# The token scales move into a filler tile, and the attention's operand comes first in its pool

## The chip, the cores and the metric

The kernel runs on one core of a Trainium2 chip. The metric is the time of one execution on the device, in microseconds (us). The time before is the median of three runs.

## The reference

A small decoder trunk on 256 tokens of width 2048, all in float32, with two layers and one shared key and value side:

```
h = x
h = h + chunked_gmlp(rmsnorm(h), w_in, w_s, w_out)        # layer 0: 2048 -> 4096, gelu, mix in chunks of 128 tokens, 2048 -> 2048
h = h + conv_ffn(rmsnorm(h), w_up, conv, w_down)          # 2048 -> 11264, causal conv of width 3, silu(gate) * value, 5632 -> 2048
k, v, c = fox_shared_kv(h, w_kvf)                         # 2048 -> 4112: keys, values, cumulative forget gates
h = h + forgetting_attention(rmsnorm(h), w_qg, w_out)     # layer 1: q and gate 2048 -> 4096, 16 heads of 128, 2048 -> 2048
h = h + conv_ffn(rmsnorm(h), w_up, conv, w_down)
out = rmsnorm(h)
```

## The kernel before

Every weight matrix is read once from HBM, in chunks of 128 x 1024 float32 (tile raw). A product keeps float32 accuracy by splitting both sides into a rounded part and a remainder in the format fp32r: ScalarE (ACT) rounds a chunk into whi, VectorE (DVE) writes the remainder into wlo, and an activation tile holds both parts side by side, 2 x 256 values for each of its 128-row slices. Three products are summed in PSUM: rounded by rounded, rounded by remainder, remainder by rounded. Class Stream runs the chunks in one written order: a chunk is loaded six ahead and split three ahead of its matmuls, and the steps of other work (generators) are advanced between chunks. So the order of instructions on every engine is fixed by the code.

There are two forms of matmul blocks, and they differ in what streams through the TensorE array and what is held in it as weights:

- feat_block (the gMLP's u and output a_out, the FFN's up, the gate b_g and the attention's output b_out): whi or wlo is held, 128 x 128 at a time, and the activation tile streams, 256 columns at a time. The tile is X1 for most, mlp_X2 for a_out, att_X2 for b_out.
- tok_blocks, short_block, with_forget and seven_block (a_in_v, b_q, the key, value and forget projections kvf, the FFN's down): the activation tile is held and whi or wlo streams, mostly 256 columns at a time. The tile is X1 for a_in_v and b_q, att_X2 for kvf, ffn_H for down.

All these matmuls go through the helper mm (line 227). A few after each call of between() are 512 columns wide.

Tiles get their place in a partition's memory from pools, stacked in the order in which each pool is opened and each tile first asked for, in steps of 32 bytes: first const (col, spare, X1, acc, rB, scales, ident, ones), then wpool (4 whi, 4 wlo, 4 raw, of 4352, 4352 and 4096 bytes), then small (place, which nothing uses, ones_r, sq and small things), then one phase pool at a time: mlp, ffn0, att, ffn1. In wpool a block form begins its data at FEAT_AT = 0 or TOK_AT = 32 elements, 0 or 128 bytes into whi and wlo.

The token scales (rcol, two columns of scales) are made by token_sums; token_rows turns them with a DVE transpose (128 x 32) and sends them through DRAM to rB, which has them along the row. In the last down block of layer 0, fourth is the first to ask for a tile of the att pool: it uses the front of att_v as scratch.

Start addresses in the built program before, bytes in each partition:

```
X1 7520   whi 43008, 47360, 51712, 56064   wlo 60416, 64768, 69120, 73472   raw 77824, ...
mlp_X2 99392   ffn0_H, ffn1_H 99392   att_v 99392   att_turned 115776, 117824   att_gain 119872   att_X2 119904
mlp_wr 164992   mlp_vr 169088   parts_qk 217056 and 219104
```

Of the kernel before, what the change touches and what calls it, by code (L numbers as in the profile page):

```python
# [10 lines left out]
F32 = mybir.dt.float32  # L11
# [6 lines left out]
P = 128  # L18
# [170 lines left out]
def build(ctx, tc, d, out):  # L189
    nc = tc.nc  # L190
    ctx.enter_context(tc.manual_schedule())
    const = ctx.enter_context(tc.tile_pool(name="const", bufs=1))
    wpool = ctx.enter_context(tc.tile_pool(name="wpool", bufs=AHEAD + 1))
    small = ctx.enter_context(tc.tile_pool(name="small", bufs=1))
# [8 lines left out]
    X1 = const.tile([P, KD, 2 * T], F32R, name="X1")  # L203
    acc = const.tile([P, T], F32, name="acc")
    rB = const.tile([P, T], F32, name="rB")
    scales = const.tile([P, 32], F32, name="scales")
    rcol = scales[:, :2]
    ident = const.tile([P, P], F32, name="ident")
    ones = const.tile([P, 2], F32, name="ones")

    small.tile([P, 144], F32, name="place")
    ones_r = small.tile([P, 2], F32R, name="ones_r")
    s = Stream(nc, wpool)
    ph = Phase(tc)
# [140 lines left out]
    def token_rows(key):  # L355

        way = dram.tile([1, T], F32, name=f"way_r{key}")
        turned = small.tile([P, 32], F32, name="turned_r", tag="turned_r")
        nc.vector.transpose(turned, scales)
        yield  # L360
        for g in range(4):
            nc.gpsimd.dma_start(way.rearrange("o (t g i) -> (o t) g i", t=2, g=4)[:, g, :],
                                turned[32 * g:32 * g + 2, :])
        yield
        yield
        nc.gpsimd.dma_start(rB, way[:1, :].to_broadcast([P, T]))

    def token_scale():
        yield
        token_sums()  # L370
        yield
        yield from token_rows("b")
# [274 lines left out]
    def sums_apart(blk):  # L647


        box = {}  # L650

        def sums(m):
            box["m"] = m
            if blk == 3:
                yield from residual_prepared()
                return
            Y = ph.temp("apart", [P, 4, T], bufs=1)
            nc.scalar.activation(Y[:, 1, :], m[:, 0, :T], AF.Copy)
            yield
            nc.vector.tensor_tensor(Y[:, 0, :], Y[:, 1, :], m[:, 0, T:], op=OP.add)  # L660
            nc.vector.tensor_tensor(Y[:, 3, :], Y[:, 0, :], m[:, 1, T:], op=OP.subtract)
            yield
            nc.vector.tensor_tensor(Y[:, 0::2, :], m[:, 1:, :T].to_broadcast([P, 2, T]), Y[:, 0::3, :], op=OP.subtract)
            box["Y"] = Y

        def fourth(ps):
            m, Y = box["m"], att("v")[:, 0, :CHUNK].rearrange("p (a b) -> p a b", a=4)
            nc.scalar.activation(Y[:, 1, :], m[:, 0, :T], AF.Copy)
            yield
            nc.vector.tensor_tensor(Y[:, 0, :], Y[:, 1, :], m[:, 0, T:], op=OP.add)  # L670
            nc.vector.tensor_tensor(Y[:, 3, :], Y[:, 0, :], m[:, 1, T:], op=OP.subtract)
            nc.vector.tensor_tensor(Y[:, 0::2, :], m[:, 1:, :T].to_broadcast([P, 2, T]), Y[:, 0::3, :], op=OP.subtract)
            Z = [Y[:, 2 * tb:2 * tb + 2, :].rearrange("p a b -> p (a b)") for tb in range(2)]
            for tb in range(2):
                nc.vector.tensor_tensor(Z[tb], Z[tb], ps(tb, 0, 512), op=OP.add)
            for tb in range(2):
                yield
                turned = blocks_turned(Z[tb].rearrange("p (h x) -> p h x", h=4))
                yield
                s.start(rows_added(blk, tb, rows_out(f"d{blk}{tb}", turned), Z[tb]))  # L680

        def done(ps):
            if blk == 3:
                yield from fourth(ps)
                return
            while "Y" not in box:
                yield
            for tb in range(2):
                z = box["Y"][:, 2 * tb:2 * tb + 2, :].rearrange("p a b -> p (a b)")
                nc.vector.tensor_tensor(z, z, ps(tb, 0, 512), op=OP.add)  # L690
                yield
                turned = blocks_turned(z.rearrange("p (h x) -> p h x", h=4))
                yield
                s.start(rows_added(blk, tb, rows_out(f"d{blk}{tb}", turned), z))
                yield

        return done, sums

    def rows_added(blk, tb, way, place):
        out_for, in_for = (2, 4) if blk == 3 else (3, 5)  # L700
        for _ in range(out_for):
            yield
        rows = place.rearrange("p (r x) -> p r x", r=4)
        rows_in(rows, way)
        for _ in range(in_for):
            yield
        hh = h[:, 4 * blk:4 * blk + 4, tb * P:(tb + 1) * P].rearrange("p h (r j) -> p r h j", r=4)
        nc.vector.tensor_tensor(hh, hh, rows.rearrange("p r (h j) -> p r h j", h=4), op=OP.add)
        state["added"] += 1

    def residual_prepared():

        for p in range(8):
            while state["added"] < 2 * (p // 2 + 1):
                yield
            for kt in (2 * p, 2 * p + 1):
                prep(X1, kt, C_BNORM)
            if p == 5:
                s.start(residual_squares())
            yield  # L720

    def residual_squares():

        for p in range(8):
            while state["added"] < 2 * (p // 2 + 1):
                yield
            sq = small.tile([P, 2, T], F32, name="sq", tag="sq", bufs=2)
            nc.scalar.activation(sq, h[:, 2 * p:2 * p + 2, :], AF.Square)
            yield
            if p == 0:  # L730
                nc.vector.tensor_tensor(acc, sq[:, 0, :], sq[:, 1, :], op=OP.add)
            else:
                for i in range(2):
                    nc.vector.tensor_tensor(acc, acc, sq[:, i, :], op=OP.add)
        yield
        token_sums()
        state["rows"] = True
        yield
        yield from token_rows("b")
# [96 lines left out]
    def input_norm():  # L836
        for _ in range(3):
            yield
        for p in range(8):
            if p % 2 == 0:  # L840
                yield
            square_into_acc(p)
        yield
        token_sums()
        state["normed"] = True
        yield
        yield from token_rows("a")
# [148 lines left out]
    def att(key):  # L996
        ph.open("att")
        shape = {"X2": [P, KD, 2 * T], "q": [P, NH, T], "k": [P, 4, 8, 4, 32], "v": [P, 2, D],
                 "ccol": [P, 2, NH], "gain": [P, 1]}[key]
        return ph.keep(key, shape, F32R if key == "X2" else F32)  # L1000

    def blocks_turned(src):


        n = src.shape[1]
        turned = ph.temp("turned", [P, 512], bufs=1 if ph.name == "ffn1" else 2)[:, :n * P].rearrange("p (c h j) -> p c h j", c=4, h=n)
        nc.vector.transpose(turned.rearrange("p c h j -> p h c j"), src.rearrange("p h (c i) -> p h c i", c=4))  # L1007
        return turned.rearrange("p c h j -> p c (h j)")

    def rows_out(key, turned):  # L1010

        way = dram.tile([4, 32, 4, turned.shape[2]], F32, name=f"way_{key}", tag=f"way_{key}")
        for r in range(4):
            nc.sync.dma_start(way[:, :, r, :].rearrange("c i x -> i c x"), turned[32 * r:32 * r + 32])
        return way
# [422 lines left out]
```

## Time and profile before

| what | us |
|---|---|
| median of 3 runs | 2257.7 (2257.54 to 2258.68) |
| the profiled execution's own time | 2257.24 |
| its span, first to last instruction | 2255.5 |
| TensorE (PE) busy | 2245.9 |
| VectorE (DVE) busy | 1674.1 |
| ScalarE (ACT) busy | 1222.6 |

The mean granted TensorE clock is 0.999. A busy TensorE is not TensorE at its peak: consecutive matmuls overlap in the records, so a matmul's duration is longer than the time from one start to the next, and that pace is what a long run of matmuls costs. In the groups by shape, a line ends in busy us, mean ns of one, and idle time before. PEld are the weight loads, one for each matmul.

### The profile page before, as it was taken

What the parts mean: (1) busy time and instruction counts of PE and PEld (TensorE: products, weight loads), DVE (VectorE), ACT (ScalarE), POOL (GpSimd) and SP (SyncE); (2) the same over time, 40 slices, a digit from 0 to 9 for tenths busy, and PEclk for the clock granted to TensorE, in tenths of its full rate; (3) what the DMA queues carried; (4) which work ended last, traced back from release to release, by engine and by line L of the source; (5) the groups of instructions that cost most, each with busy time, mean ns of one, the idle gap of its engine ahead of it and who ended that gap; (6) DMA issues with size and microseconds to landing.
All of it is one profiled execution on the core that took longest, in us unless ns stands there. A gap on an engine that the chain in (4) does not pass through costs nothing.

```text
span 2255.5 us, 45422 instructions
## 1 busy us (share of the span) xinstructions
PE 2245.9 (100%) x18558; PEld 2229.8 (99%) x18558; DVE 1674.1 (74%) x2450; ACT 1222.6 (54%) x1709; POOL 28.0 (1%) x53
## 2 busy tenths in 40 slices
PE   9999999999999999999999999999999999999998
PEld 9999999999999999999999999999999999999998
DVE  6686676666666688987877885677766666678887
ACT  6664455555555555556545764445555555555555
POOL 0000000000000000000001100000000000000000
PEclk9999999999999999999999999999999999999999
DMA  8685556565665566667788877566766666565665
GB/s 306 183 243 193 194 182 186 179 187 178 188 185 181 167 189 222 216 215 216 221 268 265 240 219 218 184 199 208 234 183 186 181 186 183 184 181 182 196 197 159
DMA packets 161489, 455.73 MB, mean 202 GB/s; under 512 B 26672, under 2 KB 49984, under 8 KB 160896
## 3 DMA queue, kind: packets, MB, share of 16 engines
q1 hardware_dynamic: 159552, 448.87, 64.1%
q0 software_dynamic: 1264, 3.41, 0.7%
q8 instruction: 145, 2.38, 0.4%
q10 hardware_dynamic: 464, 0.55, 0.1%
q14 instruction: 64, 0.52, 0.1%
HBM read 434.91 MB, written 17.84 MB: 201 GB/s over the span
## 4 chain that ended last, share of the span: by engine, by line
PE 97%; DMA 1%; DVE 1%; ACT 0%; issue 0%; SPq 0%; DVEq 0%; POOL 0%; ACTq 0%; POOLq 0%
PE ps L227 95%; PE mp L227 1%; DVE wlo L113 0%; DMA raw<-kvf_k 0%; DMA raw<-kvf_fk 0%; DMA way_q<-att_turned 0%; DMA raw<-b_q 0%; PE mp L834 0%; ACT whi L112 0%; PE mp L1284 0%; PE ps L1281 0%; DVE att_big L1104 0%; ACT sq L1093 0%; DVE att_turned L1007 0%; DVE att_hv L1095 0%
## 5 line engine op out<-in xcount | busy, mean ns | idle before, releaser
L113 DVE TENSOR_TENSOR wlo<-raw,whi 128x1024 fp32r<-128x1024 f32 (+1 forms) x724 | 878.7, 1219 | 308.5 <-ACT whi L112 301.1
L112 ACT ACTIVATE whi<-raw 128x1024 fp32r<-128x1024 f32 (+1 forms) x724 | 761.1, 1056 | 627.5 <-PE ps L227 514.4
L227 PE MATMUL ps<-X,whi 128*128 128x256 f32 (+1 forms) x6466 | 865.0, 285 | 0.0
L227 PEld LDWEIGHTS ps<-X,whi 128*128 128x128 f32 x6466 | 815.4, 188 | 7.0
L227 PE MATMUL ps<-X,wlo 128*128 128x256 f32 x3328 | 466.7, 282 | 0.0
L227 PEld LDWEIGHTS ps<-X,wlo 128*128 128x128 f32 x3328 | 429.4, 188 | 1.7
L227 PE MATMUL ps<-whi,ffn_H 128*128 128x256 f32 (+1 forms) x2124 | 356.8, 280 | 0.0
L227 PEld LDWEIGHTS ps<-whi,ffn_H 128*128 128x128 f32 x2124 | 299.1, 188 | 0.7
L227 PE MATMUL ps<-wlo,ffn_H 128*128 128x256 f32 (+1 forms) x1060 | 224.6, 280 | 0.0
L227 PE MATMUL ps<-whi,X 128*128 128x256 f32 (+1 forms) x1272 | 219.4, 282 | 0.0
L227 PEld LDWEIGHTS ps<-whi,X 128*128 128x128 f32 x1272 | 183.5, 188 | 1.4
L227 PEld LDWEIGHTS ps<-wlo,ffn_H 128*128 128x128 f32 x1060 | 167.6, 188 | 0.2
L227 PE MATMUL ps<-whi,att_X 128*128 128x256 f32 (+2 forms) x970 | 166.8, 287 | 0.0
L978 DVE SCALAR_TENSOR_TENSOR ffn_room<-ffn_room,col 128x255 f32<-128x255 f32 x352 | 161.7, 480 | 6.4
L410 DVE TENSOR_TENSOR ffn_room<-ps,rB 128x512 f32<-128x512 f32 x76 | 52.5, 691 | 132.7 <-PE ps L227 132.7
L227 PE MATMUL ps<-wlo,X 128*128 128x256 f32 (+1 forms) x634 | 142.4, 282 | 0.0
L227 PEld LDWEIGHTS ps<-whi,att_X 128*128 128x128 f32 x970 | 137.6, 188 | 3.3
L974 ACT ACTIVATE ffn_room<-ffn_room,col 128x256 f32<-128x256 f32 x176 | 96.4, 595 | 54.7 <-DVE ffn_room L410 54.7
L227 PE MATMUL ps<-wlo,att_X 128*128 128x256 f32 (+2 forms) x476 | 106.8, 289 | 0.0
L227 PEld LDWEIGHTS ps<-wlo,X 128*128 128x128 f32 x634 | 103.4, 188 | 0.4
L90 ACT ACTIVATE whi<-raw 128x768 fp32r<-128x768 f32 x54 | 45.8, 847 | 86.0 <-PE ps L227 73.5
L90 ACT ACTIVATE whi<-ffn_room 128x512 fp32r<-128x512 f32 x108 | 63.1, 627 | 31.9 <-PE ps L227 19.7
(239 smaller groups left out, 1692.7 us busy)
## 6 DMA issues: line engine op xcount, KB each, us to landing
raw<-up SPq DMA_DIRECT2D x352, 512.0 KB, 3.8
raw<-down SPq DMA_DIRECT2D x176, 512.0 KB, 4.2
raw<-a_in_u SPq DMA_DIRECT2D x32, 512.0 KB, 4.3
raw<-a_out SPq DMA_DIRECT2D x32, 512.0 KB, 3.8
raw<-b_q SPq DMA_DIRECT2D x32, 512.0 KB, 4.3
raw<-kvf_v SPq DMA_DIRECT2D x32, 512.0 KB, 4.5
raw<-b_g SPq DMA_DIRECT2D x32, 512.0 KB, 3.8
raw<-b_out SPq DMA_DIRECT2D x32, 512.0 KB, 3.9
```

The source lines that it names most:

```text
L90: self.nc.scalar.activation(hi[:, cols], src[:, cols], AF.Copy)
L112: self.nc.scalar.activation(h, raw, AF.Copy)
L113: self.nc.vector.tensor_tensor(l, raw, h.bitcast(F32), op=OP.subtract)
L227: nc.tensor.matmul(o, a, b, start=start, stop=stop, skip_group_check=True)
L410: nc.vector.tensor_tensor(a, src, rB[:, None, :].to_broadcast([P, 2, T]), op=OP.mult)
L974: nc.scalar.activation(c[:, m, :], a[:, m, :], AF.Identity, scale=w[2], bias=column(C_CONVB + l * 2 * KF + f))
L978: nc.vector.scalar_tensor_tensor(c[:, m, n:], a[:, m, :T - n], w[k], c[:, m, n:], op0=OP.mult, op1=OP.add)
```

## The change

The two tiles of the token scales are no longer allocated by themselves. scales takes the first 32 columns of the filler tile place in the small pool, and turned takes columns 64 to 95 of it. In const a tile of two columns (32 bytes with its padding) stands where scales had 128 bytes, and small is 128 bytes shorter. In fourth, att_X2 and att_gain are asked for ahead of att_v, so the att pool begins with att_X2.

```
-    scales = const.tile([P, 32], F32, name="scales")
-    rcol = scales[:, :2]
+    const.tile([P, 2], F32, name="spare_r")
...
-    small.tile([P, 144], F32, name="place")
+    place = small.tile([P, 144], F32, name="place")
+    scales = place[:, :32]
+    rcol = scales[:, :2]
...
     def token_rows(key):
-        turned = small.tile([P, 32], F32, name="turned_r", tag="turned_r")
+        turned = place[:, 64:96]
...
         def fourth(ps):
+            att("X2"), att("gain")
             m, Y = box["m"], att("v")[:, 0, :CHUNK].rearrange("p (a b) -> p a b", a=4)
```

The addresses after, bytes in each partition:

```
X1 7520   whi 42912, 47264, 51616, 55968   wlo 60320, 64672, 69024, 73376   raw 77728, ...
mlp_X2 99168   ffn0_H, ffn1_H 99168   att_X2 99168   att_gain 131936   att_v 131968   att_turned 148352, 150400
mlp_wr 164768   mlp_vr 168864   parts_qk 217056 and 219104
```

The order of instructions stays. On DVE, where token_rows runs in layer 0 (rs_t is a scratch tile of the reciprocal root, wlo<-raw the splitting of weights), before:

```order
L344 SCALAR_TENSOR_TENSOR scales<-rs_t,scales 128x2
L113 TENSOR_TENSOR wlo<-raw,whi 128x1024
L359 STREAM_TRANSPOSE turned_r<-scales 128x32
L113 TENSOR_TENSOR wlo<-raw,whi 128x1024 x13
L883 TENSOR_REDUCE ts_v<-mlp_ss 128x2
```

And now:

```order
L345 SCALAR_TENSOR_TENSOR place<-rs_t,place 128x2
L113 TENSOR_TENSOR wlo<-raw,whi 128x1024
L360 STREAM_TRANSPOSE place<-place 128x32
L113 TENSOR_TENSOR wlo<-raw,whi 128x1024 x13
L885 TENSOR_REDUCE ts_v<-mlp_ss 128x2
```

The names and line numbers are other ones, the place in the row is the same. On PE in a_out, before:

```order
L227 MATMUL ps<-mlp_X_109,wlo 128x256 x8
L227 MATMUL ps<-mlp_X_109,whi 128x256 x16
L227 MATMUL ps<-mlp_X_109,wlo 128x256 x8
L227 MATMUL ps<-mlp_X_109,whi 128x256 x16
L227 MATMUL ps<-mlp_X_109,wlo 128x256 x8
```

And now:

```order
L228 MATMUL ps<-mlp_X_109,wlo 128x256 x8
L228 MATMUL ps<-mlp_X_109,whi 128x256 x16
L228 MATMUL ps<-mlp_X_109,wlo 128x256 x8
L228 MATMUL ps<-mlp_X_109,whi 128x256 x16
L228 MATMUL ps<-mlp_X_109,wlo 128x256 x8
```

Only the line number has moved; the tiles behind the names lie elsewhere.

## The prediction

> **What bounds the kernel now.** I read the busy shares first, then who waited for whom on TensorE, then the chain that ended last cut into stages, then the groups of matmuls by shape. The lines say that TensorE is busy all the time, that the chain is made of its matmuls, and that it hardly waits: 2.0 us in all.
>
> ```profile
> span 2255.5 us, 45422 instructions
> PE 2245.9 (100%) x18558; PEld 2229.8 (99%) x18558; DVE 1674.1 (74%) x2450; ACT 1222.6 (54%) x1709; POOL 28.0 (1%) x53
> ...
> PE 97%; DMA 1%; DVE 1%; ACT 0%; issue 0%; SPq 0%; DVEq 0%; POOL 0%; ACTq 0%; POOLq 0%
> ```
>
> ```profile
> PE mp L834 <- POOL ident L1325: 1.5, 1, 1.5
> PE mp L1148 <- ACT att_f L1143: 0.5, 1, 0.5
> ```
>
> So the time is the number of matmuls times the pace at which one follows another. That pace is read from the chain, cut to a stretch in which only one kind of matmul runs (columns: start in us, length in us, what, how many). In this order: a_out, up0, b_out, then b_q, kvf_k, kvf_v, down0.
>
> ```profile
> 239.96 20.06 PE ps L227 x177
> 309.92 115.20 PE ps L227 x960
> 1424.99 80.04 PE ps L227 x667
> 1031.99 38.04 PE ps L227 x323
> 1149.97 40.13 PE ps L227 x344
> 1204.90 15.19 PE ps L227 x129
> 794.91 85.15 PE ps L227 x723
> ```
>
> Length over count gives ns per matmul: a_out 113.3, up0 120.0, b_out 120.0, b_q 117.8, kvf_k 116.7, kvf_v 117.8, down0 117.8. All are 256 columns wide on 128 x 128 weights, and nothing waits. The first three even run the same function, feat_block, with the same PSUM pattern. What differs between a_out at 113.3 and up0 or b_out at 120.0 is the tile that streams: mlp_X2 in the first, X1 and att_X2 in the others. The mean duration of one matmul says the same for every group, 276 ns where the pace is 113.3, 279 to 280 where it is 116.7 to 117.8, 282 where it is 120.0:
>
> ```profile
> L227 PE MATMUL ps<-X,whi 128*128 128x256 f32 x6276 | 817.2, 282 | 0.0
> L227 PE MATMUL ps<-X,wlo 128*128 128x256 f32 x3328 | 466.7, 282 | 0.0
> L227 PE MATMUL ps<-whi,ffn_H 128*128 128x256 f32 x2112 | 353.0, 279 | 0.0
> L227 PE MATMUL ps<-wlo,ffn_H 128*128 128x256 f32 x1052 | 221.4, 279 | 0.0
> L227 PE MATMUL ps<-whi,X 128*128 128x256 f32 x1248 | 211.6, 280 | 0.0
> L227 PE MATMUL ps<-whi,att_X 128*128 128x256 f32 x852 | 137.3, 279 | 0.0
> L227 PE MATMUL ps<-wlo,X 128*128 128x256 f32 x620 | 137.0, 279 | 0.0
> L227 PE MATMUL ps<-wlo,att_X 128*128 128x256 f32 x408 | 83.4, 279 | 0.0
> L227 PE MATMUL ps<-att_X,whi 128*128 128x256 f32 x512 | 66.6, 282 | 0.0
> L227 PE MATMUL ps<-mlp_X,whi 128*128 128x256 f32 x512 | 63.2, 276 | 0.0
> L227 PE MATMUL ps<-X,whi 128*128 128x512 f32 x190 | 50.9, 397 | 0.0
> L227 PE MATMUL ps<-att_X,wlo 128*128 128x256 f32 x256 | 35.9, 282 | 0.0
> L227 PE MATMUL ps<-mlp_X,wlo 128*128 128x256 f32 x256 | 34.2, 276 | 0.0
> L227 PE MATMUL ps<-whi,ffn_H 128*128 128x512 f32 x12 | 4.1, 396 | 0.0
> L227 PE MATMUL mp<-parts_qk,parts_qk 128*128 128x256 f32 x48 | 7.0, 282 | 0.0
> L227 PE MATMUL ps<-mlp_vr,mlp_wr 128*128 128x256 f32 x48 | 6.3, 281 | 0.0
> ```
>
> The first input named is the one that streams, the second the one held as weights. To see what the groups have in common I take the addresses listed ahead (whi and wlo share every remainder below) and form the offset: start of the streaming operand less start of the held one, modulo 128 bytes. All index steps within a stage are multiples of 256 bytes, so one stage has one offset. up0 and b_out have 96, and run at 120.0. a_out has 64, and runs at 113.3. b_q and kvf have 32, and run at 116.7 or 117.8. down0 has 64, and runs at 117.8. The head products parts_qk and the mixing product mlp_vr by mlp_wr have 0, and last 281 to 282 ns like the 120.0 groups. Within each of the two block forms the offset 64 is at or near the best, and 0 and 96 are worst.
>
> **The change part by part.** No instruction is added, removed or moved: the order of all five engines reads the same apart from names. The three edits work through addresses alone.
>
> Scales out of the constants: everything allocated behind them moves down 96 bytes, X1 stays. The offset of X1 as the streaming operand goes from 96 to 64 (it was -35488, it is -35392 bytes to whi), as the held one from 32 to 64.
>
> Turned scales out of the small pool: the phase pools come 128 bytes nearer to whi. Modulo 128 nothing changes for mlp_X2 and ffn_H, they keep 64. Modulo 256 they go from 64 to 192, and X1 ends at 192 too; no row here has 192, which is why a rival below stands on it.
>
> att_X2 to the front of its pool: it no longer lies behind att_v, two turned tiles and att_gain (20512 bytes, 32 modulo 128), so its offset goes from 96 to 64 streaming and from 32 to 64 held.
>
> Term 1, feat blocks with X1 and att_X2: 6276 + 3328 + 512 + 256 = 10372 matmuls at 120.0. I take the pace of a_out, the one stage of the same form at offset 64: 10372 x (120.0 - 113.3) ns = 69.2 us saved. Bounds: a_out's 113.3 is the best pace in the trace, and down0 at the same offset shows 117.8, which would save 10372 x 2.2 = 23 us; staying at 120.0 saves nothing.
>
> Term 2, token blocks with X1 or att_X2 held: 1248 + 620 + 852 + 408 = 3128 matmuls now at 116.7 or 117.8. Their nearest row at offset 64 is down0, of the same role, at 117.8: between 0 and 3128 x 1.1 = 3.4 us lost, I take the middle, 1.7. The other end is 113.3: 3128 x 3.4 to 4.5, or 10 to 14 us saved.
>
> Term 3, mlp_X2 and ffn_H: offset kept, 0. The bounds are the other rows: a_out at 120.0 loses 768 x 6.7 = 5.1 us, down at 113.3 saves (2112 + 1052 and some 210 into the mp banks) 3374 x 4.5 = 15 us, at 120.0 loses 3374 x 2.2 = 7.5 us.
>
> Term 4, the 512-wide ones: 190 last 397 ns at offset 96 and 12 last 396 at 64, so 0; if one 512-wide gained as much as two 256-wide ones, 190 x 13.4 = 2.5 us.
>
> Term 5, the scales in the filler: the same DVE and ACT instructions on another address, and the queue of POOL issues the same loads from turned. They run beside matmuls; DVE has slack in the closest stretches (32.01 of 38, 35.40 of 40, 75.51 of 85 us):
>
> ```profile
> 5.00:57.00 52.00, 52.00 (x426) 51.13 (x425) 36.58 (x52) 32.38 (x48) 2.01 (x1) 1.00 0.89 315
> 310.00:425.00 115.00, 115.00 (x961) 115.00 (x960) 81.79 (x117) 62.00 (x85) 0.00 (x0) 1.00 0.61 188
> 1032.00:1070.00 38.00, 38.00 (x325) 38.00 (x325) 32.01 (x53) 24.68 (x37) 0.00 (x0) 1.00 0.74 223
> 1150.00:1190.00 40.00, 40.00 (x345) 40.00 (x345) 35.40 (x68) 17.31 (x19) 0.30 (x1) 1.00 0.85 274
> 795.00:880.00 85.00, 85.00 (x724) 85.00 (x723) 75.51 (x97) 44.15 (x53) 0.00 (x0) 1.00 0.65 203
> ```
>
> (Columns: window, length, busy us and count of PE, PEld, DVE, ACT, POOL, granted clock, DMA share, GB/s.) The clock is 1.00 in each, so it explains no pace. A faster TensorE asks DVE for 81.79 us of work in about 109 instead of 115, and the weight loads for a DMA share of 0.65 instead of 0.61: both stay covered. Where the share is already 0.89, in the first 52 us, only token blocks run, which term 2 leaves alone; if loads to the moved raw tiles were slower and paced that stretch by the 5 parts in 100 that I allow, it would cost 3 us. Taken as 0.
>
> Sum: -69.2 + 1.7 = -67.5. The profiled execution took 2257.24 us, against a median of 2257.7 for the three runs, 0.02% apart; 2257.24 - 67.5 = 2189.7, so 2190.
>
> One rule speaks against all of this. The Trainium skill, TensorE: Matmul & The Clock Gate, section Step-by-step: what each phase is for, says that TensorE has two independent read ports, and that loading the next weights takes nothing from the running matmul. By it the place of one operand relative to the other is worth 0 and the time stays at 2257. This trace does not agree that place is free: the same form runs at 113.3 in a_out and at 120.0 in b_out.
>
> **The rivals.**
> Token blocks gain as well. a_out and down0 have the same offset, but in a_out the held side starts at 0 modulo 128 and the streaming one at 64, in down0 the other way round. If that, and not the form of the block, makes 113.3 against 117.8, the new places (32 and 96) may give 113.3 everywhere: 69.2 + 12 + 15 + up to 2.5 is 98.7 us, 2159. For it speaks that kvf_k and kvf_v differ at equal addresses, so the token form is not tied to one pace; against it, that no token stretch shows 113.3.
>
> Half the gain. All stages fall to down0's 117.8: 23 us saved, a_out loses 768 x 4.5 = 3.5: 2238.
>
> No change. Offset 192 modulo 256 behaves like the old ones, or the pace hangs on something that isn't moved (also the page's case): 2257.
>
> Slower. What counts is that the streaming operand itself starts on a multiple of 64 bytes. mlp_X2 does now (99392) and has the best pace; X1, att_X2 and parts_qk don't and are at 120.0; whi and wlo in the token blocks do (43136) and are between. After the change every one of them starts at 32 modulo 64. Then all go to 120.0: a_out loses 5.1 us, down 7.5, token blocks 3128 x 2.2 to 3.3 = 8.7, and X1 gains nothing: 2279. Against it stands mlp_vr by mlp_wr, where both start on multiples of 128 and the matmul still lasts 281 ns, as the offset rule has it. It decides from the first matmuls of a_out: 276 or 282 ns.
>
> **How the numbers follow.** My forecast of 2190 gets 0.38: it takes each stage to the row of its own form. Token blocks too, 0.25. Half, 0.10. No change, 0.08. Slower, 0.19, since it orders the seven stretches as well as the offset does, and only mlp_vr by mlp_wr goes against it. A difference under 0.2% is about what a measurement of this kernel can't tell from none. Faster then has 0.73, same 0.08, slower 0.19. The range leaves the slower case out and reaches from a little below 2159 to 2262 at the far side of no change: 2150 to 2262. The forecast's own range is 2184 to 2196, by terms 2 to 5.
>
> **What would show it.** Right: mean durations of ps<-X,whi and ps<-att_X,whi fall from 282 to 276, up0 runs at 113.3 ns per matmul, a_out stays at 276, down at 279, TensorE still waits for next to nothing. Wrong: a_out rises to 282 (the slower case), X1 stays at 282, or TensorE begins to wait for wlo or for raw, which would mean that DVE or the loads take over as the bound.

## The result and the profile after

The changed kernel takes 2161.05 us (median, 2160.71 to 2163.4) where the one before takes 2257.54 us in the same series; the ratio is 0.9575 with a 95% interval of 0.9561 to 0.9589. That is 96.5 us less, within the forecast range, but 29 us below the forecast of 2190, outside the forecast's own range of 2184 to 2196, and 2 us above the 2159 of the rival in which the token blocks gain as well.

The page of the changed kernel: still all TensorE, with the same instruction counts, and the chain is made of matmuls even more than before.

```profile
span 2159.0 us, 45422 instructions
PE 2149.3 (100%) x18558; PEld 2133.5 (99%) x18558; DVE 1668.9 (77%) x2450; ACT 1221.4 (57%) x1709; POOL 28.1 (1%) x53
...
q1 hardware_dynamic: 159552, 448.87, 65.2%
...
PE 99%; DMA 0%; DVE 0%; ACT 0%; issue 0%; POOL 0%; DVEq 0%; ACTq 0%; POOLq 0%
```

The chain in the same stages, a_out, up0, b_out, b_q, kvf_k, kvf_v, down0 (start us, length us, what, count):

```profile
234.96 20.06 PE ps L228 x177
299.96 110.05 PE ps L228 x971
1369.90 75.14 PE ps L228 x663
984.92 35.13 PE ps L228 x310
1104.94 40.13 PE ps L228 x352
1154.96 18.13 PE ps L228 x160
764.94 30.15 PE ps L228 x266
```

Length over count: 113.3 ns in every one but kvf_k, where two intervals between matmuls are twice as long and make it 114.0. The seven stages that ran at four different paces now run at one. The groups of matmuls by shape say it in mean durations, 276 to 277 ns for all of the 256-wide ones that moved. The 512-wide ones still last 397 ns, and the head products parts_qk, whose offset is still 0, last 283 where they lasted 282:

```profile
L228 PE MATMUL ps<-X,whi 128*128 128x256 f32 x6276 | 776.3, 276 | 0.0
L228 PE MATMUL ps<-whi,ffn_H 128*128 128x256 f32 x2112 | 343.6, 276 | 0.0
L228 PE MATMUL ps<-whi,X 128*128 128x256 f32 x1248 | 206.3, 277 | 0.0
L228 PE MATMUL ps<-whi,att_X 128*128 128x256 f32 x852 | 134.4, 277 | 0.0
L228 PE MATMUL ps<-mlp_X,whi 128*128 128x256 f32 x512 | 63.3, 276 | 0.0
L228 PE MATMUL ps<-att_X,whi 128*128 128x256 f32 x512 | 63.3, 276 | 0.0
L228 PE MATMUL ps<-X,whi 128*128 128x512 f32 x190 | 50.7, 397 | 0.0
L228 PE MATMUL mp<-parts_qk,parts_qk 128*128 128x256 f32 x48 | 7.0, 283 | 0.0
```

### The profile page after: what moved, and what is told of

The parts are those of the page before. It is cut to its first block, busy times and chain, and to the rows that moved or that the text cites. A ratio compares the mean times of both kernels' runs of the same rounds, so it can differ in the third digit from the quotient of the medians.

```text
span 2159.0 us, 45422 instructions
## 1 busy us (share of the span) xinstructions
PE 2149.3 (100%) x18558; PEld 2133.5 (99%) x18558; DVE 1668.9 (77%) x2450; ACT 1221.4 (57%) x1709; POOL 28.1 (1%) x53
## 3 DMA queue, kind: packets, MB, share of 16 engines
q1 hardware_dynamic: 159552, 448.87, 65.2%
## 4 chain that ended last, share of the span: by engine, by line
PE 99%; DMA 0%; DVE 0%; ACT 0%; issue 0%; POOL 0%; DVEq 0%; ACTq 0%; POOLq 0%
PE ps L228 96%; PE mp L228 2%; DMA raw<-kvf_k 0%; PE mp L836 0%; PE mp L1286 0%; PE ps L1283 0%; ACT sq L460 0%; ACT whi L112 0%; DVE h_h L803 0%; DVE h_h L459 0%; DVE h_h L797 0%; PE mp L431 0%; ACT fin_t L789 0%; DVE fin_t L793 0%; DVE wlo L113 0%
## 5 line engine op out<-in xcount | busy, mean ns | idle before, releaser
L228 PE MATMUL ps<-X,whi 128*128 128x256 f32 (+1 forms) x6466 | 824.0, 280 | 0.0
L228 PEld LDWEIGHTS ps<-X,whi 128*128 128x128 f32 x6466 | 775.3, 188 | 6.7
L228 PE MATMUL ps<-X,wlo 128*128 128x256 f32 x3328 | 445.5, 277 | 0.0
L228 PEld LDWEIGHTS ps<-X,wlo 128*128 128x128 f32 x3328 | 409.8, 188 | 1.7
L228 PE MATMUL ps<-whi,ffn_H 128*128 128x256 f32 (+1 forms) x2124 | 347.4, 277 | 0.0
L228 PEld LDWEIGHTS ps<-whi,ffn_H 128*128 128x128 f32 x2124 | 292.9, 188 | 0.7
L228 PE MATMUL ps<-whi,X 128*128 128x256 f32 (+1 forms) x1272 | 214.1, 279 | 0.0
L411 DVE TENSOR_TENSOR ffn_room<-ps,rB 128x512 f32<-128x512 f32 x76 | 52.5, 691 | 113.7 <-PE ps L228 113.7
```

The lines of the kernel that those rows point to most:

```text
L228: nc.tensor.matmul(o, a, b, start=start, stop=stop, skip_group_check=True)
L411: nc.vector.tensor_tensor(a, src, rB[:, None, :].to_broadcast([P, 2, T]), op=OP.mult)
```

## The experiments

Offset means, as in the prediction, the start of the streaming operand less the start of the held one, but modulo 256 bytes from here on. In the kernel before it is 96 for X1 and att_X2 streaming, 32 for them held, 64 for mlp_X2 and ffn_H; in the changed kernel it is 192 for all four tiles.

**Absolute place or offset.** Two kernels from the changed one:

```
 e1: const.tile([P, 16], ..., name="spare")  ->  const.tile([P, 40], ..., name="spare")
 e2: FEAT_AT, TOK_AT = 0, 32                 ->  FEAT_AT, TOK_AT = 32, 0
```

> The changed kernel with the spare tile in const 96 bytes larger: every operand of the matmuls moves up by 96 bytes, so all offsets stay at 192 modulo 256 (64 modulo 128), but X1, mlp_X2, ffn_H and att_X2 now start at 192, whi at 0 in the feat blocks and at 128 in the token blocks. Theory S (the signed offset, modulo 256, decides): all stages stay at 113.3 ns per matmul, 2161 us. Theory H (offset 64 modulo 128, and a streaming operand that starts at 0 modulo 128 costs 4.4 ns, as in down before): feat blocks 113.3, token blocks 117.8, some 6700 x 4.45 ns = 30 us more, 2191 us.

> The changed kernel with FEAT_AT, TOK_AT = 32, 0 in place of 0, 32: the data in whi and wlo begin 128 bytes later in the feat blocks and 128 bytes earlier in the token blocks. All starts stay as they are modulo 128; all offsets go from 192 to 64 modulo 256. Theory S: feat blocks stay at 113.3 (offset 64, as a_out before), token blocks go to 117.8 (offset 64, as down before), 2191 us. Theory H: nothing changes, 2161 us.

e1 took 2162.93 us, ratio to before 0.9579 (0.9563 to 0.9595). Its up0 and down0 in the chain:

```profile
299.89 100.20 PE ps L228 x883
769.97 80.13 PE ps L228 x707
```

Both are at 113.3 to 113.5 ns, though every operand starts 96 bytes elsewhere, and the streaming one of the token blocks on a multiple of 128. So a move of all operands together costs nothing that shows (2162.93 against 2161.05 us), theory H is out, and with it the rival by which starts on multiples of 64 bytes matter. e2 took 2229.38 us, ratio 0.9874 (0.9859 to 0.9889). So 64 and 192 differ and modulo 128 is too coarse. But S missed by 38 us as well, and the trace shows why. Its chain in a_out, up0, b_out, then in kvf_k and the first value block:

```profile
195.91 84.09 PE ps L228 x714
309.89 110.12 PE ps L228 x935
1399.95 80.13 PE ps L228 x707
1139.97 45.11 PE ps L228 x383
1195.96 16.09 PE ps L228 x142
```

That is 117.8, 117.8, 113.3, 117.8 and 113.3 ns, all at offset 64. The feat blocks do not keep the 113.3 that a_out had in the kernel before; b_out has it here, a_out doesn't. At offset 64 a stretch runs at one of two paces, whatever its form, and each of these five keeps its pace through its window.

**The parts of the change.** e3 leaves out the line that puts att_X2 first; e4 is the kernel before with only that line; e5 gives the turned scales their own tile again; e6 puts scales back into const:

```
 e3: changed kernel    -            att("X2"), att("gain")
 e4: kernel before     +            att("X2"), att("gain")
 e5: changed kernel    -        turned = place[:, 64:96]
                       +        turned = small.tile([P, 32], F32, name="turned_r", tag="turned_r")
 e6: changed kernel    -    const.tile([P, 2], F32, name="spare_r")
                       +    scales = const.tile([P, 32], F32, name="scales")
```

> The changed kernel without the line that asks for att_X2 ahead of att_v: att_X2 starts at 128 modulo 256, its offset is 224 (96 modulo 128) streaming in b_out and 160 (32 modulo 128) held in kvf. Both S and H: b_out goes to 120.0 as in before (768 x 6.7 ns = 5.1 us), kvf to 116.7 or 117.8 (1260 x 3.3 to 4.4 ns = 4.2 to 5.5 us), 2170 to 2172 us. If the order in the att pool is worth nothing: 2161 us.

> The kernel before with only that line added: att_X2 starts at 64 modulo 256 as mlp_X2 and ffn_H do, offset 64 in both roles; all else as before. Both S and H: b_out falls from 120.0 to 113.3 (5.1 us), kvf goes to 117.8 as down (0 to 1.4 us more), 2253 us against 2257.5. If the gain needs the scales moved too: 2257.5 us.

> The changed kernel with the turned scales back in a tile of their own (128 bytes in the small pool): the phase pools lie 128 bytes further from whi, so mlp_X2, ffn_H and att_X2 go from offset 192 to 64 modulo 256, in both roles, while X1 keeps 192. Theory S2 (offset 64 has two paces, 113.3 and 117.8, and a stretch keeps the one that it is entered in; 192 has 113.3 alone): X1 stays at 113.3; the 6170 matmuls of the other tiles run at either, so between 2161 us and 6170 x 4.45 ns = 27 us more, 2188 us, and every long stretch shows one of the two paces and none between. Theory H (modulo 128 decides): 2161 us, all at 113.3.

> The changed kernel with scales back in const (128 bytes there, the turned scales still in place): whi and all behind it lie 96 bytes further from X1, so X1 has offset 96 streaming and 32 held as before; mlp_X2, ffn_H and att_X2 move along with whi and keep 192. If the offset modulo 256 decides: up, u, the gate at 120.0 (9604 x 6.65 ns = 64 us), a_in_v and b_q at 116.7 or 117.8 (2060 x 3.3 to 4.4 ns = 7 to 9 us), a_out, b_out, kvf and down at 113.3: 2232 to 2234 us. If the steps of the change only work together, more is lost: up to 2257 us.

e3 took 2170.79 us (ratio 0.9615, 0.9601 to 0.963), the expected time: the order in the att pool is worth some 10 us beside the other two edits. The paces behind it were not the expected ones. b_out runs at 118.3 instead of 120.0, and kvf_k at 118.7 instead of 116.7 or 117.8 (its rows stand under the map below); the two misses nearly cancel. e4 took 2255.67 us (ratio 0.999, 0.9981 to 1.0), 2 us less than before where some 4 were expected, and at the edge of what the runs can tell from nothing: alone the edit brings att_X2 to offset 64, and b_out goes only to 117.8. Its chain in a_out, kvf_k and b_out shows both paces at the same offset 64 in one kernel:

```profile
204.97 80.13 PE ps L227 x705
1149.93 40.16 PE ps L227 x341
1411.96 83.15 PE ps L227 x706
```

113.7 (the last 4.5 us of this window are up0 at 120.0 already; cut at 280 us, a_out has 663 matmuls in 75.14 us, 113.3) against 117.8 and 117.8. e5 took 2174.36 us (ratio 0.9634, 0.9618 to 0.965), 13 us above the changed kernel, inside the span that S2 left and against H. Its chain in a_out, the first down block, a later one and b_out:

```profile
189.96 80.09 PE ps L228 x680
762.95 40.16 PE ps L228 x341
813.99 8.05 PE ps L228 x71
1365.97 80.09 PE ps L228 x680
```

117.8, 117.8, 113.4, 117.8: ffn_H changes from one pace to the other near the end of the first down block, at one and the same offset. It does so at 808.6 us, where something new begins in the row of matmuls: the down blocks also hold sums that are kept in X1, at offset 192 here, and from there on these products stand in between those on ffn_H. e6 took 2231.89 us (ratio 0.9887, 0.9874 to 0.9901), as expected: the 96 bytes of scales are worth 71 us of the 96.5. Its up0 and its a_out:

```profile
319.93 110.16 PE ps L227 x918
201.99 78.09 PE ps L227 x689
```

120.0 for X1, back at offset 96, and 113.3 for mlp_X2. Taken away one at a time from the changed kernel, the three edits cost 9.7, 13.3 and 70.8 us, 93.8 together.

**A map of the offsets.** Three kernels from the changed one move mlp_X2 and ffn_H by the length of place, and att_X2 by a filler ahead of it, so that each shows up to four new offsets:

```
 m1: place [P, 120], filler [P, 8]    m2: place [P, 136], filler [P, 24]    m3: place [P, 168], filler [P, 8]
 +            ph.open("att")
 +            ph.pool.tile([P, 8], F32, name="att_fill")
              att("X2"), att("gain")
```

> A map of offsets: the changed kernel with place 96 bytes shorter and a filler of 32 bytes ahead of att_X2. mlp_X2 and ffn_H start at 0, att_X2 at 32 modulo 256; whi and X1 as in the changed kernel. Offsets: a_out 96, b_out 128, down 32, kvf 0. If the offset modulo 256 alone decides: a_out 120.0 (5.1 us), down 116.7 or 117.8 (11 to 15 us), kvf 120.0 (8 us), b_out, whose offset no run had yet, 113.3 to 120.0 (0 to 5.1 us): 2185 to 2195 us. If a multiple of 128 is free: b_out and kvf at 113.3.

> A map of offsets: the changed kernel with place 32 bytes shorter and a filler of 96 bytes ahead of att_X2. mlp_X2 and ffn_H start at 64, att_X2 at 160 modulo 256. Offsets: a_out 160, b_out 0, down 224, kvf 128. If the offset modulo 256 alone decides: a_out 118.7 as kvf in the kernel with the values first (4.1 us), b_out 120.0 (5.1 us), down 118.3 as b_out there (17 us), kvf as b_out of the first map (0 to 8 us): 2187 to 2196 us. If the roles matter too, a_out and down differ from these by over 1 ns.

> A map of offsets: the changed kernel with place 96 bytes longer and a filler of 32 bytes ahead of att_X2. mlp_X2 and ffn_H start at 192, att_X2 at 224 modulo 256. Offsets: a_out 32, b_out 64, down 96, kvf 64. If the offset modulo 256 alone decides: a_out 116.7 or 117.8 (2.6 to 3.4 us), down 120.0 (22 us), b_out and kvf each at 113.3 or 117.8 (0 to 9 us): 2185 to 2196 us. If the roles matter too, down is off 120.0 by over 1 ns.

They took 2191.25, 2192.8 and 2194.86 us, one run each, all within what was expected. Their chains, a_out, b_out, kvf_k, down0 of m1, then of m2, then of m3:

```profile
189.97 85.08 PE ps L228 x709
1375.88 84.14 PE ps L228 x709
1114.88 45.12 PE ps L228 x376
764.94 40.16 PE ps L228 x341
```

```profile
189.92 80.14 PE ps L228 x683
1375.91 82.20 PE ps L228 x685
1114.89 45.21 PE ps L228 x381
761.93 38.10 PE ps L228 x322
```

```profile
189.96 80.15 PE ps L228 x687
1376.00 82.09 PE ps L228 x697
1119.89 40.16 PE ps L228 x341
761.93 38.16 PE ps L228 x318
```

Put together with the runs above, ns per 256-wide matmul (512-wide ones stand among them in all of these kernels as in the changed one):

| offset modulo 256 | pace, ns | seen in |
|---|---|---|
| 0 | 120.0 | m1 kvf_k, m2 b_out |
| 32 | 116.7 or 117.8 | kernel before b_q and kvf_k, m1 down0, m3 a_out |
| 64 | 113.3 or 117.8 | kernel before a_out and down0, e2, e4, e5, m3 |
| 96 | 120.0 | kernel before up0, e6 up0, m1 a_out, m3 down0 |
| 128 | 118.7 | m1 b_out, m2 kvf_k |
| 160 | 117.3, 118.7 | m2 a_out; kvf_k of e3 |
| 192 | 113.3; 117.8 behind some groups of wide ones, for up to 17 us | changed kernel, e1 |
| 224 | 118.3 | m2 down0; b_out of e3 |

The two rows of e3 are these, kvf_k and b_out:

```profile
1109.97 40.11 PE ps L228 x338
1374.94 75.14 PE ps L228 x635
```

At 0, 96, 128 and 224 the role, the tile and the form of the block don't show: both forms have the same pace. At 160 a_out of m2 is 1.3 ns below kvf_k of e3, which is the sign that the expectation named for a part of the roles; whether it is that or again two paces at one offset can't be told from one stage each. The clearest row for the offset is one stage in which two tiles take turns: in down of e6, between 800 and 1010 us, matmuls on X1 (offset 32) follow one another at 116.5 ns from start to start, and those on ffn_H (offset 192) between them at 113.3.

**What picks the pace at 64.** Many changes of pace at 64 and 192 stand where the 512-wide matmuls are, eight and then two after each call of between(). Two kernels do without them, and one keeps two of the ten:

```
 e7: changed kernel, wide_next() returns 0
 e8: e2, wide_next() returns 0
 e9: changed kernel, state["wide"] = [8, 2]  ->  [2]
```

> The changed kernel without 512-wide matmuls: wide_next gives 0, so each of the 338 becomes two of 256. A 512-wide one takes 35 steps of 6.67 ns (233.3 ns) in the changed kernel's long runs, two 256-wide ones 34 (226.7). If nothing else hangs on them: 338 x 6.7 ns = 2.2 us less, 2159 us, and fewer additions on DVE. If they cover something after the short matmuls that they follow, TensorE waits there instead: 2161 us or more.

> FEAT_AT, TOK_AT = 32, 0 as in e2 (all offsets 64) and no 512-wide matmuls. It asks what picks one of the two paces at offset 64. If the 512-wide ones do, stretches that they no longer part keep one pace across, and several stretches have another pace than in e2: any time from 2161 to 2240 us, 113.3 and 117.8 still the only paces. If something else does: stretch for stretch as in e2, 2227 us (2229 less 2.2).

> The changed kernel with only the first two matmuls 512 wide after each call of between(), instead of eight and then two: 68 of them in place of 338. Without any, long stretches at offset 192 ran at 117.8 ns and the kernel took 2199.6 us; with all, at 113.3 and 2161 us. If two are enough to bring a stretch to 113.3: 270 x 6.7 ns = 1.8 us less than the changed kernel, 2159 us. If their number matters: stretches at 117.8 come back, between 2165 and 2200 us.

e7 missed: 2199.63 us, ratio 0.9744 (0.973 to 0.9757), 39 us slower than the changed kernel instead of 2 faster. TensorE waits for nothing new. It is the pace again, this time at offset 192. a_out, up0 and up1 of e7:

```profile
191.90 80.13 PE ps L228 x707
289.91 470.17 PE ps L228 x3992
1479.98 470.05 PE ps L228 x3991
```

113.3 in a_out, 117.8 through both long windows of up0 and up1, where the changed kernel has 113.3. The first 8 us of up0 still run at 113.3 (63 matmuls in 7.14 us); the pace changes at 284.3 us, where the two short products mp<-sq,ones_r stand in between, and does not come back before the end of up0. So 192 has the same two paces as 64. e8 took 2238.59 us (ratio 0.9917, 0.9899 to 0.9935); its up0 and its kvf_k:

```profile
299.97 470.05 PE ps L228 x3991
1141.92 46.13 PE ps L228 x407
```

117.8 and 113.3; in e2 kvf_k has 117.8, and b_out, 113.3 in e2, is at 117.8 here. So the wide matmuls have a part in which pace a stretch gets, at 64 and at 192. e9 took 2182.42 us (ratio 0.9665, 0.9652 to 0.9679), between the two; its up0 and down0:

```profile
299.97 110.05 PE ps L228 x971
757.90 40.16 PE ps L228 x341
```

113.3 and 117.8 at one offset. up0 runs at 117.8 behind its first pair of wide matmuls (107 in 12.60 us) and at 113.3 behind the second, 15 us later; down0 has one pair, and stays slow behind it. In the changed kernel a pair follows nearly every eight, and the starts of the matmuls in its trace show what that is worth: behind the 34 groups of eight the pace is 113.3 in 24 cases and 117.8 in 10, behind the 33 pairs it is 113.3 in every one. In e2, at offset 64, it is 117.8 behind 27 of the 33 pairs. None of these three kernels beats the changed one.

## Why the prediction was right, and where it was wrong

The mechanism is shown in the main: no instruction moves, TensorE waits for as little as before, and the time is the count of matmuls times a pace that hangs on the offset of the two operands. Two steps of the working failed all the same: it took the offset modulo 128 where modulo 256 counts, and it gave each offset and form one pace, where 32, 64 and 192 have two; at 64 and 192 what stands ahead in the row of matmuls has a part in which.

Term 1, the feat blocks with X1 and att_X2, 69.2 us: right in size, and partly by luck. They went from 120.0 to 113.3. I read a_out's 113.3 as the pace of that form at offset 64; e4 has b_out at 117.8 with that form and that offset, and in e2 up0 and a_out have it too. The offset that the change gives them is not 64 but 192 modulo 256, and had it been 64, term 1 could have been short by up to 10372 x 4.4 ns = 46 us, as e2 shows for most of these matmuls. At 192 too up0 and up1 run at 113.3 only with the wide matmuls among them, as e7 shows.

Term 2, the token blocks, +1.7 us: wrong, and of the wrong sign. They went to 113.3, the other bound of that term, 10 to 14 us less.

Term 3, ffn_H, 0: wrong. down fell from 117.8 to 113.3, 3374 x 4.5 = 15 us, again the other bound. mlp_X2 stayed, as said. Terms 2 and 3 are one mistake: down0's 117.8 was taken for the pace of the token form at offset 64, when it was the slow one of two paces that either form can have. The bounds caught it, the choice between them did not. 69.2 + 12 + 15 is 96, what was measured.

Terms 4 and 5: right. The 512-wide matmuls kept their 397 ns; the queue share of the loads is 65.2%, against 64.1% in a span 4.5% longer, and TensorE waits for no load, so the moved raw tiles cost nothing that shows.

The rule of the Trainium skill that I weighed (TensorE: Matmul & The Clock Gate, section Step-by-step: what each phase is for: two independent read ports, loading the next weights takes nothing from the running matmul) would have given no change. The map does not agree that the place is free: 113.3 to 120.0 ns, by where the two operands start relative to each other. Whether it is the loading of the weights that takes the difference, no run here shows.

The rivals: "Token blocks gain as well" has the right time and half of the right reason. That the token form is not tied to one pace is so, but its condition, where each operand itself starts modulo 128, is refuted by e1, in which the token blocks have the starts that down0 had before, modulo 128, and run at 113.3. The slower one is refuted by e1 and by the changed kernel itself, whose streaming operands all start at 32 modulo 64. "No change" asked the right question, whether 192 differs from 64, and got the wrong answer. "Half the gain" did not come about here, but it is what e8 shows: 117.8 nearly everywhere and 2238.59 us, where the rival said 2238.

Open: why the offset matters inside TensorE or its memory ports, and why a pair of wide matmuls leads to the fast pace at 192 and mostly to the slow one at 64. No run here looks inside.

## What to carry to other kernels

When TensorE never waits, compare the pace of equal matmuls between stages before anything else: a stage that runs the same form some per cent faster is a lead, and here it was the place of its operands that differed. A tile that is added or removed ahead of such operands moves them all: here 96 bytes of scratch are worth 71 us, 3%, and a filler can keep the offset. And one stage at a good pace does not say that its setting has that pace alone: look for a second stage with the same setting, as a_out and down0 were here, and take their disagreement seriously.

## What was not expected of the hardware

Long stretches of identical matmuls have two steady paces at one placement, 113.3 and 117.8 ns, and a stretch of 3992 matmuls stays in the slow one from end to end with nothing to wait for. The 512-wide matmuls after each interruption turn out to be worth 38.6 us at offset 192 (e7 against the changed kernel) and 9.2 us at 64 (e8 against e2) with the same products computed; at 192 it is by bringing the stretches behind them to the fast pace.
